# Two blocks of each feed-forward network as one seven-product step over both token tiles

## The chip, the core and the metric

The program runs on one core of one Trainium2 chip. The metric is the device time of one execution in microseconds (us). TensorE (PE) multiplies matrices, VectorE (DVE) and ScalarE (ACT) do elementwise work, GpSimd (POOL) has a handful of small operations, and SyncE (SP) issues transfers. Each engine runs its own instructions in their written order; an instruction that depends on another engine waits for a semaphore, and whatever stands behind it on that engine waits too.

## The reference

256 tokens of width 1024 pass through two layers. Each layer is a feed-forward network (FFN), a mixer (state-space branch and chunked attention) and a second FFN, all of it float32:

```python
def swiglu(h, w_gate, w_up, w_down):
    return (jax.nn.silu(h @ w_gate) * (h @ w_up)) @ w_down
...
    for l in range(DEPTH):
        g = norm_gains[l]
        f1 = swiglu(rmsnorm(x, g[0]), ffn_w_gate[l, 0], ffn_w_up[l, 0], ffn_w_down[l, 0])
        x = x + 0.5 * rmsnorm(f1, g[1])
        m = hybrid_mixer(rmsnorm(x, g[2]), w_in[l], ...)
        x = x + rmsnorm(m, g[3])
        f2 = swiglu(rmsnorm(x, g[4]), ffn_w_gate[l, 1], ffn_w_up[l, 1], ffn_w_down[l, 1])
        x = x + 0.5 * rmsnorm(f2, g[5])
```

The hidden width of an FFN is 2816; gate and up weights are 1024 x 2816, the down weight 2816 x 1024.

## The kernel before

**Tiles.** The tokens form two tiles, t = 0 and t = 1, of 128 rows. A float32 product is made of three fast ones: both operands are cut into a high part and a remainder (`hi` and `lo` for activations, `wh` and `wl` for weights), and `mm_two_k` (L468) issues hi x wh, hi x wl and lo x wh, each a 128x128 by 128x512 matmul into one bank of PSUM.

**Weights.** All weights lie in HBM as 368 chunks of 128 x 1024 (512 KB). `weight` (L443) brings one in: a transfer that SP issues into a `raw` buffer, then on ACT `wh` = raw rounded (L358), then on DVE `wl` = raw - wh (L365). There are 4 `raw` buffers and 8 each of `wh` and `wl`. Every chunk is used by both tiles, tile 1 up to three chunks behind tile 0 (`LAG`), with 6 matmuls for each tile.

**An FFN** (`ffn`, L581, called once for each tile) cuts the hidden width into six blocks, `N_BLK`, five of 512 and one of 256. For a block of 512 it takes 4 chunks of gate weights and 4 of up weights (each chunk holds 256 of the 1024 input rows), applies silu and the product (L586, L594), transposes the result into `hi` and `lo` (`t_split`), and multiplies the block before it by 4 chunks of the down weights into two banks that collect over the FFN (`gemm_wide`). A block thus has 12 chunks, 144 matmuls of 512 columns and 8 transposes. At an FFN's two ends `boundary` (L554) makes the norms and the next input, one tile after the other.

**The order** is set before anything runs. `Graph.schedule` (L197) gives every operation a due time that follows from the matmuls' places (`take`, L460) less a margin for each stream of work (`MARGIN`), lays all engines out in time with costs written into the program, buffer counts (`SLOTS`) included, and the program is emitted in the order of the start times. The chip then only keeps the order within each engine. `prep` (L622) makes constants for the state-space branch; its stream may run far ahead of its use.

Of the kernel before, what the change touches and what calls it, by code (L numbers as in the profile page):

```python
# [12 lines left out]
F32 = mybir.dt.float32  # L13
# [16 lines left out]
N_BLK = (512, 512, 512, 512, 512, 256)  # L30
FFN_CHUNKS = 66
# [4 lines left out]
SLOTS = {"blk": 28, "ps": 8, "wh": 8, "wl": 8, "raw": 4, "gain": 2,  # L36
# [4 lines left out]
MARGIN = {"conv": 7.558, "conv0": 3.423, "task": 7.748, "att0": 37.576, "s50": 37.749, "att1": 28.585, "s51": 29.753, "prep": 111.598}  # L41
# [10 lines left out]
DMA_RATE = 350e3  # L52

# [8 lines left out]
class View:  # L62
# [50 lines left out]
    def ap(self):  # L113
        t = self.buf.tile
        for s in self.steps:
            t = s(t)
        return t

# [10 lines left out]
class Graph:  # L129
# [62 lines left out]
    def latency(self, a, b):  # L192
        if a.eng == "dma":
            return DMA_LAT if b.eng != "dma" else 0.0
        return LAT.get((a.eng, b.eng), HOP)

    def schedule(self):  # L197
# [23 lines left out]
        while left:  # L221
# [90 lines left out]
class Kern:  # L312
    def __init__(self, g, x, g0, gains, wall, sp, bias, out):
# [4 lines left out]
        self.chunk = [0, 0]  # L318
        self.last_raw = None
# [46 lines left out]

    def copy(self, out, a):
# [24 lines left out]
    def mm(self, out, lhsT, rhs, start, stop):  # L392
# [3 lines left out]
        elif m == 32:  # L396
            cost = 0.05
        else:
            cost = max(0.2, n / 592)
        return self.g.op("pe", cost, [out], [lhsT, rhs], lambda: self.nc.tensor.matmul(  # L400
            out.ap(), lhsT=lhsT.ap(), rhs=rhs.ap(), start=start, stop=stop))
# [40 lines left out]

    def weight(self, i):  # L443
        if i not in self.ws:
# [3 lines left out]
            raw = g.buf("raw", [P, 1024])  # L448
            wh, wl = g.buf("wh", [P, 1024], F32R), g.buf("wl", [P, 1024], F32R)
            parts = [slice(0, 512), slice(512, 1024)] if i < 2 else [slice(0, 1024)]  # L450
            for s in parts:
                self.last_raw = self.dma(raw[:, s], self.w_d[i][:, s], after=[self.last_raw] if self.last_raw else [])
            for s in parts:
                self.act(wh[:, s], raw[:, s], AF.Copy)
                self.tt(wl[:, s], raw[:, s], wh[:, s].bitcast(F32), ALU.subtract)
            self.ws[i] = (wh, wl)
# [3 lines left out]
    def take(self, t):  # L460
# [4 lines left out]
        self.mode("main", "main", (i + t * min(LAG, 1 + i // 2)) * 2 * TAU + t * TAU)  # L465
        return w

    def mm_two_k(self, bank, xs, w, first, last):  # L468
        wh, wl = w
        for i, (xh, _) in enumerate(xs):  # L470
            s = slice(i * 512, (i + 1) * 512)
            self.mm(bank, xh, wh[:, s], first and i == 0, False)
            self.mm(bank, xh, wl[:, s], False, False)
        for i, (_, xl) in enumerate(xs):
            self.mm(bank, xl, wh[:, i * 512:(i + 1) * 512], False, last and i == len(xs) - 1)

    def gemm(self, t, xs):
# [6 lines left out]
        return bank  # L484

# [29 lines left out]
    def to_lhs(self, halves):  # L515
# [7 lines left out]
        return [p for h in range(2) for p in zip(self.cols(nh[h]), self.cols(nl[h]))]  # L523
# [6 lines left out]
    def first_norm(self, t):  # L530
# [9 lines left out]
        return [p for h in range(2) for p in zip(self.cols(nh[h]), self.cols(nl[h]))], None  # L540
# [40 lines left out]
    def ffn(self, t, l, f, normed):  # L581
        ipost = 1 if f == 0 else 5
        nxt = (l, 2) if f == 0 else (l + 1, 0)
        xs, rs = normed
        acc = (self.ps(), self.ps())
        pend, first = None, True  # L586
        for b, wd in enumerate(N_BLK):
            sil, h = self.blk(), self.blk()
            gb = self.gemm(t, xs)
            if rs is None:  # L590
                rs = self.row_scale(t, [self.g.ops[self.mark[(t, 2)]]])
            self.act(sil[:, :wd], gb[:, :wd], AF.Silu, scale=rs)
            up = self.gemm(t, xs) if wd == 512 else gb[:, wd:]
            self.stt(h[:, :wd], up, rs, sil[:, :wd], ALU.mult, ALU.mult)  # L594
# [549 lines left out]
```

## Time and profile before

| | |
|---|---|
| time, median of 3 runs | 1153.77 us (1153.56 to 1154.09) |
| profiled execution, first to last instruction | 1151.6 us |
| the same executions' time beyond the span | 1153.77 - 1151.6 = 2.2 us |
| PE busy | 1140.8 us, 99% |
| DVE busy | 788.6 us, 68% |
| ACT busy | 606.3 us, 53% |
| POOL busy | 19.8 us, 2% |
| transfers' share of the 16 DMA engines | 53.7% |

Busy is the time in which an engine had an instruction under way; matmuls are pipelined, so one lasts longer (0.4 us) than the distance to the next (some 0.23 us), and the distance is what counts.

### The profile page before, as it was taken

To read this page: it belongs to the slowest core of one execution; us is meant where nothing else is said; L and a number is where in the kernel's file an instruction comes from. 1 tells how busy PE (TensorE), PEld (TensorE's weight loads), DVE (VectorE), ACT (ScalarE), POOL (GpSimd) and SP (SyncE) were. 2 spreads that over 40 slices of the span, in tenths; PEclk is the share of its full clock that TensorE was granted. 3 is DMA by queue.
4 is the path that set the end of the run, shared out by engine and by line. 5 is a ranking of instruction groups with operands and counts; after the bars stand their busy time and mean duration, and the time that the engine had idled before them with its cause. 6 is when DMAs were issued, how large, how long until landed. Compare 5 with 4: busy or idle time off the path is not lost.

```text
span 1151.6 us, 15538 instructions
## 1 busy us (share of the span) xinstructions
PE 1140.8 (99%) x5872; PEld 914.0 (79%) x5872; DVE 788.6 (68%) x1190; ACT 606.3 (53%) x894; POOL 19.8 (2%) x53
## 2 busy tenths in 40 slices
PE   8999999999999999999999999999999999999997
PEld 7887888877788888888888878887777888888886
DVE  6995557896958854655799734578779678544553
ACT  6565445648555554444555643455685446444442
POOL 1000000000000000000000000000000000000000
PEclk9999999999999999999999999999999999999999
DMA  8754565553255665555565546654534565555551
GB/s 291 252 195 159 183 219 166 181 164 130 86 189 178 207 200 184 186 182 184 187 220 193 184 150 200 204 177 147 166 110 145 184 198 163 192 192 181 190 165 37
DMA packets 60267, 205.02 MB, mean 178 GB/s; under 512 B 7072, under 2 KB 7840, under 8 KB 60192
## 3 DMA queue, kind: packets, MB, share of 16 engines
q1 hardware_dynamic: 60192, 204.03, 53.7%
q8 instruction: 46, 0.75, 0.3%
q14 instruction: 29, 0.24, 0.1%
HBM read 202.96 MB, written 1.05 MB: 177 GB/s over the span
## 4 chain that ended last, share of the span: by engine, by line
PE 94%; ACT 4%; issue 1%; DMA 0%; SPq 0%; DVE 0%; POOLq 0%; POOL 0%; DVEq 0%
PE ps L400 89%; PE ps L414 4%; ACT utz L358 2%; PE ps L406 1%; ACT blk L358 1%; ACT wh L358 1%; DMA x<-in_x_dram 0%; SPq L341 0%; DVE x L380 0%; POOLq L1139 0%; POOL s L376 0%; DVEq L1139 0%; DVE s L388 0%; POOLq L376 0%
## 5 line engine op out<-in xcount | busy, mean ns | idle before, releaser
L400 PE MATMUL ps<-wh,blk 128*128 128x512 f32 x2944 | 916.4, 400 | 0.0
L400 PEld LDWEIGHTS ps<-wh,blk 128*128 128x128 f32 x2944 | 548.0, 188 | 122.6 <-issue 0.3
L365 DVE TENSOR_TENSOR wl<-raw,wh 128x1024 fp32r<-128x1024 f32 (+1 forms) x370 | 448.7, 1217 | 281.9 <-ACT wh L358 280.6
L358 ACT ACTIVATE wh<-raw 128x1024 fp32r<-128x1024 f32 (+1 forms) x370 | 389.7, 1055 | 374.5 <-PE ps L400 334.1
L400 PE MATMUL ps<-wl,blk 128*128 128x512 f32 x1472 | 551.7, 399 | 0.0
L400 PEld LDWEIGHTS ps<-wl,blk 128*128 128x128 f32 x1472 | 274.8, 188 | 61.1 <-issue 0.3
L358 ACT ACTIVATE blk<-ps 128x512 fp32r<-128x512 f32 (+3 forms) x136 | 78.1, 583 | 121.5 <-PE ps L414 103.3
L365 DVE TENSOR_TENSOR blk<-ps,blk 128x512 fp32r<-128x512 f32 (+2 forms) x104 | 69.0, 666 | 36.1 <-ACT blk L358 34.9
L414 PE MATMUL ps<-ident,blk 128*128 128x128 f32 x432 | 76.8, 273 | 0.2
L414 PEld LDWEIGHTS ps<-ident,blk 128*128 128x128 f32 x432 | 57.0, 140 | 20.1 <-ACT blk L358 1.0
L358 ACT ACTIVATE blk<-ps,s 128x512 f32<-128x512 f32 (+1 forms) x80 | 52.5, 658 | 27.6 <-PE ps L400 25.6
L380 DVE SCALAR_TENSOR_TENSOR blk<-ps,s,blk 128x512 f32<-128x512 f32 (+1 forms) x48 | 33.8, 703 | 15.3 <-PE ps L400 11.5
L376 POOL TENSOR_TENSOR s<-s,mhalf 128x1 f32<-128x1 f32 x24 | 13.8, 574 | 804.0 <-DVE s L388 799.1
L358 ACT ACTIVATE blk<-blk,s 128x128 f32<-128x128 f32 (+1 forms) x64 | 25.8, 444 | 0.0
L400 PEld LDWEIGHTS ps<-utz,bt 128*128 128x128 f32 x128 | 18.1, 191 | 4.0 <-ACT utz L358 2.8
L365 DVE TENSOR_TENSOR blk<-blk,blk 128x512 f32<-128x512 f32 (+3 forms) x38 | 21.1, 577 | 0.1
L358 ACT ACTIVATE utz<-blk 32x128 f32<-32x128 f32 x64 | 20.1, 314 | 1.0
L358 ACT ACTIVATE blk<-blk 64x128 f32<-64x128 f32 (+2 forms) x44 | 17.1, 393 | 6.5 <-DVE blk L380 6.0
L365 DVE TENSOR_TENSOR blk<-blk,e 128x512 f32<-128x512 f32 x32 | 20.3, 677 | 0.0
L400 PE MATMUL ps<-utz,bt 128*128 128x128 f32 x128 | 19.2, 278 | 1.0 <-ACT utz L358 0.8
L365 DVE TENSOR_TENSOR blk<-ps,e 128x512 f32<-128x512 f32 x32 | 19.9, 677 | 0.0
L856 DVE TENSOR_TENSOR_SCAN blk<-mt,blk 128x512 f32<-128x512 f32 x16 | 18.6, 1203 | 0.0
(106 smaller groups left out, 349.2 us busy)
## 6 DMA issues: line engine op xcount, KB each, us to landing
raw<-in_wall_dram SPq DMA_DIRECT2D x366, 512.0 KB, 3.5
gain<-in_gains_dram SPq DMA_DIRECT2D x22, 256.0 KB, 4.6
blk<-in_bias_dram SPq DMA_DIRECT2D x8, 256.0 KB, 5.0
raw<-in_wall_dram SPq DMA_DIRECT2D x4, 256.0 KB, 3.5
blk<-in_sp_dram SPq DMA_DIRECT2D x4, 256.0 KB, 4.0
x<-in_x_dram SPq DMA_DIRECT2D x3, 256.0 KB, 5.5
out_dram<-x SPq DMA_DIRECT2D x2, 256.0 KB, 2.0
out_dram<-x SPq DMA_DIRECT2D x2, 192.0 KB, 2.1
```

The costliest lines, as they stand in the source:

```text
L358: self.nc.scalar.activation(out=out.ap(), in_=in_.ap(), func=func, **k)
L365: lambda: self.nc.vector.tensor_tensor(out=out.ap(), in0=a.ap(), in1=b.ap(), op=op))
L376: lambda: self.nc.gpsimd.tensor_tensor(out=out.ap(), in0=a.ap(), in1=b.ap(), op=ALU.pow))
L380: return self.g.op("dve", cost, [out], [a, s, b], lambda: self.nc.vector.scalar_tensor_tensor(out=out.ap(), in0=a.ap(), scalar=ap(s), in1= ...
L400: return self.g.op("pe", cost, [out], [lhsT, rhs], lambda: self.nc.tensor.matmul(out.ap(), lhsT=lhsT.ap(), rhs=rhs.ap(), start=start, stop ...
L406: self.nc.tensor.matmul(out.ap(), lhsT=lhsT.ap(), rhs=rhs.ap(), start=start, stop=stop)
L414: lambda o=o, s=s: self.nc.tensor.transpose(o.ap(), s.ap(), self.ident.ap()))
L856: self.g.op("dve", 0.6, [o], [mt, z], lambda o=o, z=z: self.nc.vector.tensor_tensor_scan(out=o.ap(), data0=mt.ap(), data1=z.ap(), initial= ...
```

## The change

Blocks 1 and 3 of each of the four FFNs, eight blocks in all, are now computed for both tiles at once. Take the two tiles as the rows of a 2 x 2 block matrix A whose columns are the two halves of the 1024 inputs, and gate and up weights as the columns of a 2 x 2 block matrix B with the same halves as rows. The four blocks of A B (gate and up of both tiles) need 8 block products in the usual way. `seven` computes them from 7 products of sums of the blocks (Winograd's form of Strassen's scheme). A product is 12 matmuls, so a block has 84 + 48 = 132 matmuls of 512 columns in place of 96 + 48 = 144; its 8 transposes stay.

The sums of A are made once for each FFN on DVE and ACT (`sums`). The sums of B are made in the `raw` buffers: ACT multiplies four chunks by -1 in place (`minus`), and eight transfers with an adding destination, issued by POOL from SBUF to SBUF (`add_to`, 512 KB each), add chunks to chunks. Seven pairs of `wh` and `wl` are then made from the 8 loaded gate and up chunks, where there were four: 14 conversions in place of 8. The products' sums (`u2`, `u4`, `h`) are five more DVE operations on 128x512, and one ACT copy (`k1`) takes a product out of a bank that goes on collecting. `raw` has 9 buffers, `wh` and `wl` 7. Two padded buffers that were kept all along (`uTz`) are now made and cleared by POOL for each use. `prep` has a margin of 40.

```diff
+SEVEN = (((1, 3), (1, 3)), ((1, 3), (1, 3)))
-SLOTS = {"blk": 28, "ps": 8, "wh": 8, "wl": 8, "raw": 4, "gain": 2,
+SLOTS = {"blk": 28, "ps": 8, "wh": 7, "wl": 7, "raw": 9, "gain": 2,
-MARGIN = {"conv": 7.558, "conv0": 3.423, "task": 7.748, "att0": 37.576, "s50": 37.749, "att1": 28.585, "s51": 29.753, "prep": 111.598}
+MARGIN = {"conv": 7.558, "conv0": 3.423, "task": 7.748, "att0": 37.576, "s50": 37.749, "att1": 28.585, "sums": 8.0, "s51": 29.753, "prep": 40.0}
+ADD_LAT = 4.6
...
+    def add_to(self, out, in_):
+        return self.g.op("pool", 0.9, [out], [out, in_],
+                         lambda: self.nc.gpsimd.dma_start(out=out.ap(), in_=in_.ap(), accum_op=ALU.add), func="dma")
...
+    def sums(self, xs):
+        self.mode("sums", "bulk")
+        a = []
+        for t in range(2):
+            for hi, lo in xs[t].full:
+                r = self.blk()
+                self.tt(r, hi.bitcast(F32), lo.bitcast(F32), ALU.add)
+                a.append(r)
+        a11, a12, a21, a22 = a
+        self.tt(a22, a21, a22, ALU.add)
+        self.tt(a21, a11, a21, ALU.subtract)
+        self.tt(a11, a22, a11, ALU.subtract)
+        self.tt(a12, a12, a11, ALU.subtract)
+        out = []
+        for r, k in ((a22, -1.0), (a11, 1.0), (a21, 1.0), (a12, 1.0)):
+            hi, lo = self.blk(F32R), self.blk(F32R)
+            self.act(hi, r, AF.Copy, scale=k)
+            self.stt(lo, r, k, hi.bitcast(F32), ALU.mult, ALU.subtract)
+            out.append((hi, lo))
...
+    def seven(self, b, xs, rs, s, acc, pend, first):
...
+        def minus(raws):
+            for r in raws:
+                self.act(r, r, AF.Copy, scale=-1.0)
+
+        def add(to, raws):
+            for o, r in zip(to, raws):
+                self.add_to(o, r)
+
+        b11 = [self.load(i), self.load(i + 1)]
+        w1 = conv(b11)
+        self.weight(i + 2)
+        b21 = [self.load(i + 3), self.load(i + 4)]
+        w2 = conv(b21)
+        minus(b21)
+        b12 = [self.load(i + 5), self.load(i + 6)]
+        minus(b12)
+        add(b11, b12)
+        w5 = conv(b11)
+        b22 = [self.load(i + 7), self.load(i + 8)]
+        add(b12, b22)
+        add(b11, b22)
+        w6 = conv(b11)
+        self.weight(i + 9)
+        w7 = conv(b12)
+        w3 = conv(b22)
+        self.weight(i + 10)
+        add(b21, b11)
+        w4 = conv(b21)
+        self.weight(i + 11)
...
+        prod(0, p1, a11, w1, True)
+        k1 = self.blk()
+        self.act(k1, p1, AF.Copy)
+        down(2, 0)
+        prod(4, p1, a12, w2, False)
...
+        prod(6, p5, s1, w5, True)
+        prod(8, p6, s2, w6, True)
+        u2, u4 = self.blk(), self.blk()
+        self.tt(u2, p6, k1, ALU.add)
+        self.tt(u4, p5, u2, ALU.add)
+        down(10, 1)
...
+        prod(12, p7, s3, w7, True)
+        self.tt(u4, p7, u4, ALU.add)
+        prod(14, p5, s4, w3, False)
...
+        down(16, 2)
+        prod(18, p7, a22, w4, False)
...
+        down(20, 3)
+        return [self.t_split(h[t], 4) for t in range(2)]
...
+            if b in SEVEN[l][f]:
+                if s is None:
+                    s = self.sums(xs)
+                pend = self.seven(b, xs, rs, s, acc, pend, first)
...
-        self.uTz = [self.own(f"utz{i}", [P, 2, 2, 2, 64]) for i in range(2)]
+        uz = [self.blk() for _ in range(2)]
+        for z in uz:
+            self.memset("pool", z, 0.0)
```

Three pieces show how instructions stand, in block 1 of the second FFN. First POOL. In the program before, the four inverse roots of the boundaries around that block follow each other with nothing between (the four `s1` rows; the two before them clear the scan's start):

```order
L346 MEMSET st0_369_141 128x16
L346 MEMSET st1_370_143 128x16
L376 TENSOR_TENSOR s1_667_3634<-s1_666_3627,mhalf_2_74 128x1
L376 TENSOR_TENSOR s1_781_3740<-s1_780_3732,mhalf_2_74 128x1
L376 TENSOR_TENSOR s1_677_3786<-s1_676_3781,mhalf_2_74 128x1
L376 TENSOR_TENSOR s1_791_3859<-s1_790_3856,mhalf_2_74 128x1
```

Now the eight adding transfers of block 1 stand behind the last of them. raw_892 and raw_893 are the two chunks of b11, 907 and 908 those of b12, 913 and 914 of b22, 901 and 902 of b21:

```order
L391 TENSOR_TENSOR s1_835_3943<-s1_834_3936,mhalf_2_74 128x1
L380 DMA raw_892_3675<-raw_907_3793 128x1024
L380 DMA raw_893_3702<-raw_908_3814 128x1024
L380 DMA raw_907_3793<-raw_913_3854 128x1024
L380 DMA raw_908_3814<-raw_914_3941 128x1024
L380 DMA raw_892_3675<-raw_913_3854 128x1024
L380 DMA raw_893_3702<-raw_914_3941 128x1024
L380 DMA raw_901_3758<-raw_892_3675 128x1024
L380 DMA raw_902_3779<-raw_893_3702 128x1024
```

POOL has eight transfers in each of the eight blocks where it had none, and the fifth and sixth, which complete the sums for the product `w6`, come after four others.

Second PE, at block 1's second tile. Before, tile 1's gate product goes over the same weights that tile 0 used (wh_842, wh_845), between down products (ps_792 and ps_793 collect them):

```order
L400 MATMUL ps_1070_4034<-wh_842_3881,blk_782_3766 128x512
L400 MATMUL ps_1070_4034<-wl_843_3889,blk_782_3766 128x512
L400 MATMUL ps_1070_4034<-wh_842_3881,blk_782_3766 128x512
L400 MATMUL ps_1070_4034<-wl_843_3889,blk_782_3766 128x512
L400 MATMUL ps_1070_4034<-wh_842_3881,blk_784_3775 128x512 x2
L400 MATMUL ps_792_4043<-wh_857_3960,blk_823_3982 128x512
L400 MATMUL ps_793_4049<-wh_857_3960,blk_823_3982 128x512
```

Now the product on `w5` (the second chunk's pair is wh_911, wl_912) is followed at once by the first matmul on `w6` (wh_915), whose low part wl_916 comes seven matmuls later:

```order
L416 MATMUL ps_944_4120<-wh_911_4046,blk_882_3990 128x512
L416 MATMUL ps_944_4120<-wl_912_4062,blk_882_3990 128x512
L416 MATMUL ps_944_4120<-wh_911_4046,blk_883_4017 128x512 x2
L416 MATMUL ps_945_4149<-wh_915_4135,blk_884_4091 128x512
L416 MATMUL ps_836_4060<-wh_920_4058,blk_869_3998 128x512
L416 MATMUL ps_837_4064<-wh_920_4058,blk_869_3998 128x512
L416 MATMUL ps_836_4060<-wl_921_4087,blk_869_3998 128x512
L416 MATMUL ps_837_4064<-wl_921_4087,blk_869_3998 128x512
L416 MATMUL ps_836_4060<-wh_920_4058,blk_870_4010 128x512
L416 MATMUL ps_837_4064<-wh_920_4058,blk_870_4010 128x512
L416 MATMUL ps_948_4167<-wh_922_4101,blk_886_4032 128x512
L416 MATMUL ps_945_4149<-wl_916_4151,blk_884_4091 128x512
```

Behind the first `w6` matmul stand the six of a down chunk (wh_920) and one of `w7` (wh_922), and then the `w6` product goes on.

Third ACT in the same block. Before, conversions of freshly loaded chunks follow one another, each from a buffer of its own:

```order
L358 ACTIVATE wh_872_4047<-raw_871_3978 128x1024
L358 ACTIVATE blk_1065_4061<-ps_1064_4051 128x512
L358 ACTIVATE wh_875_4075<-raw_874_4006 128x1024
L358 ACTIVATE wh_878_4093<-raw_877_4021 128x1024
L358 ACTIVATE wh_881_4111<-raw_880_4045 128x1024
```

Now the two conversions for `w5` (from raw_892 and raw_893 after the first add) stand ahead of the copy `k1` out of the bank ps_940:

```order
L369 ACTIVATE wh_909_4036<-raw_892_3675 128x1024
L369 ACTIVATE wh_911_4046<-raw_893_3702 128x1024
L369 ACTIVATE blk_941_4054<-ps_940_3975 128x512
L369 ACTIVATE wh_920_4058<-raw_919_4004 128x1024
L369 ACTIVATE raw_901_3758<-raw_901_3758 128x1024
L369 ACTIVATE wh_926_4078<-raw_913_3854 128x1024
```

PE's next matmul into ps_940, the start of the product on `w2`, follows that copy.

## Rows read from the trace of the kernel before

**Rows 1.** The page's part 1: span; busy us of each engine.
```profile
span 1151.6 us, 15538 instructions
PE 1140.8 (99%) x5872; PEld 914.0 (79%) x5872; DVE 788.6 (68%) x1190; ACT 606.3 (53%) x894; POOL 19.8 (2%) x53
```

**Rows 2.** The page's part 4: the chain that ended last, shares by engine.
```profile
PE 94%; ACT 4%; issue 1%; DMA 0%; SPq 0%; DVE 0%; POOLq 0%; POOL 0%; DVEq 0%
```

**Rows 3.** Waits of the whole run: who waited for whom, us, times, longest.
```profile
ACT wh L358 <- PE ps L400: 334.1, 237, 3.0
DVE wl L365 <- ACT wh L358: 280.6, 257, 3.2
...
ACT wh L358 <- DMA raw<-in_wall_dram: 17.5, 19, 1.8
```

**Rows 4.** The chain in time, second FFN: start us, us, what.
```profile
454.25 9.02 PE ps L400 x39
...
464.18 23.74 PE ps L400 x102
...
488.58 9.09 PE ps L400 x39
...
498.57 23.70 PE ps L400 x102
...
522.94 9.03 PE ps L400 x39
```

**Rows 5.** Windows of two blocks: busy us of each engine, clock, DMA share, GB/s.
```profile
464.18:498.57 34.39, 34.39 (x153) 27.76 (x153) 21.98 (x53) 16.09 (x17) 0.00 (x0) 1.00 0.55 184
498.57:532.87 34.30, 34.30 (x153) 27.75 (x153) 17.46 (x17) 15.07 (x16) 0.00 (x0) 1.00 0.54 182
```

**Rows 6.** Groups by line and shape: busy us, mean ns, then idle before.
```profile
L365 DVE TENSOR_TENSOR wl<-raw,wh 128x1024 fp32r<-128x1024 f32 x366 | 446.0, 1223 | 278.9 <-ACT wh L358 277.7 <-issue 0.3
L358 ACT ACTIVATE wh<-raw 128x1024 fp32r<-128x1024 f32 x366 | 387.2, 1059 | 371.6 <-PE ps L400 334.1 <-issue 15.8 <-DMA raw<-in_wall_dram 14.6
...
L358 ACT ACTIVATE blk<-ps 128x512 f32<-128x512 f32 x28 | 15.8, 594 | 13.4 <-PE ps L414 9.8 <-PE ps L400 3.6
```

**Rows 7.** Timeline of DVE at a boundary: start us, us, what.
```profile
382.06 2.35 DVE L365 TENSOR_TENSOR wl<-raw,wh 128x1024 fp32r<-128x1024 f32 x2
384.33 0.68 DVE L365 TENSOR_TENSOR blk<-ps,blk 128x512 fp32r<-128x512 f32 x1
384.93 0.74 DVE L380 SCALAR_TENSOR_TENSOR blk<-blk,s,blk 128x512 f32<-128x512 f32 x1
385.59 1.22 DVE L365 TENSOR_TENSOR wl<-raw,wh 128x1024 fp32r<-128x1024 f32 x1
```

**Rows 8.** Windows around the second FFN's start, columns as in rows 5.
```profile
380.00:390.00 10.00, 10.00 (x49) 8.18 (x48) 9.63 (x15) 5.49 (x8) 0.55 (x1) 1.00 0.59 197
390.00:400.00 10.00, 10.00 (x49) 8.16 (x48) 9.65 (x15) 7.49 (x13) 1.10 (x2) 1.00 0.48 155
```

**Rows 9.** Queues and issues, whole run: share of 16 engines; KB, us to landing.
```profile
q1 hardware_dynamic: 60192, 204.03, 53.7%
...
raw<-in_wall_dram SPq DMA_DIRECT2D x366, 512.0 KB, 3.5
...
raw<-in_wall_dram SPq DMA_DIRECT2D x4, 256.0 KB, 3.5
...
out_dram<-x SPq DMA_DIRECT2D x2, 256.0 KB, 2.0
```

**Rows 10.** The same view from 10 to 60 us, the first FFN.
```profile
q1 hardware_dynamic: 4265, 13.68, 78.7%
...
raw<-in_wall_dram SPq DMA_DIRECT2D x22, 512.0 KB, 4.7
```

**Rows 11.** Windows of the first FFN, columns as in rows 5.
```profile
20.00:30.00 10.00, 10.00 (x45) 8.10 (x44) 7.54 (x17) 6.68 (x10) 0.55 (x1) 1.00 0.97 330
30.00:40.00 10.00, 10.00 (x45) 8.12 (x44) 9.61 (x32) 6.38 (x7) 0.00 (x0) 1.00 0.87 293
```

**Rows 12.** POOL's line L376: duration ns min/median/max, first and last start.
```profile
L376 POOL TENSOR_TENSOR s<-s,mhalf x24: 549/550/1108, 16.1 to 1146.4; 128x1 f32<-128x1 f32 x24
```

More of the change, by code (lines that the diff above doesn't have):

```diff
@@ L441, in cols, with load, halves @@
         return [t[:, i * P:(i + 1) * P] for i in range(n)]
+    def load(self, i, parts=(slice(0, 1024),)):
+        raw = self.g.buf("raw", [P, 1024])
+        for s in parts:
+            self.last_raw = self.dma(raw[:, s], self.w_d[i][:, s], after=[self.last_raw] if self.last_raw else [])
+        return raw
+    def halves(self, raw, parts=(slice(0, 1024),)):
+        wh, wl = self.g.buf("wh", [P, 1024], F32R), self.g.buf("wl", [P, 1024], F32R)
+        for s in parts:
+            self.act(wh[:, s], raw[:, s], AF.Copy)
+            self.tt(wl[:, s], raw[:, s], wh[:, s].bitcast(F32), ALU.subtract)
+        return wh, wl
     def weight(self, i):
@@ L447, in weight @@
             self.mode("conv" if i >= 6 else "conv0", "main")
[L448 to L456, printed above, removed]
+            parts = (slice(0, 512), slice(512, 1024)) if i < 2 else (slice(0, 1024),)
+            self.ws[i] = self.halves(self.load(i, parts), parts)
             g.stream, g.rank, g.due = keep
@@ L522, in to_lhs @@
         self.split(*trios)
-        return [p for h in range(2) for p in zip(self.cols(nh[h]), self.cols(nl[h]))]
+        return Lhs(nh, nl, [p for h in range(2) for p in zip(self.cols(nh[h]), self.cols(nl[h]))])
     def row_scale(self, t, after=()):
@@ L539, in first_norm @@
                 self.stt(lo, b, gk, hi.bitcast(F32), ALU.mult, ALU.subtract)
-        return [p for h in range(2) for p in zip(self.cols(nh[h]), self.cols(nl[h]))], None
+        return Lhs(nh, nl, [p for h in range(2) for p in zip(self.cols(nh[h]), self.cols(nl[h]))]), None
     def pre_gain(self, t, l, i):
@@ L599, in ffn @@
                     self.gain(*nxt)
-            if b == len(N_BLK) - 1:
-                pre = self.pre_gain(t, *nxt)
-            if pend is not None:
-                self.gemm_wide(t, acc, pend, first, False)
-                first = False
-            pend = res
-        self.gemm_wide(t, acc, pend, False, True)
-        return self.boundary(t, l, ipost, acc, 1.0 / 16, 4.0 * EPS, *nxt, pre)
+        out = []
+        for t in range(2):
+            self.gemm_wide(t, acc[t], pend[t], False, True)
+            out.append(self.boundary(t, l, ipost, acc[t], 1.0 / 16, 4.0 * EPS, *nxt, pre[t]))
+        return out
     def persistent(self):
```

130 lines of the change are left out of this document (100 added, 30 removed).

## The prediction

> **What bounds the kernel now.** I read the page's busy times first, then the chain that ended last, then the waits, and only then the stage that the change touches. PE is busy for 1140.8 of 1151.6 us [rows 1] and carries 94% of the chain that ended last [rows 2]; the granted clock is 1.00 in every window shown. The waits say that weights are ready early: ACT's conversions stand still for 334.1 us until PE gives a buffer back, and for only 17.5 us until a load lands [rows 3]. So the supply runs ahead as far as the buffers let it, and time is the number of matmuls times their distance. In the second FFN two whole blocks take 34.39 and 34.30 us [rows 5], and the chain's stretches put one 512-column matmul at 23.74 / 102 = 0.2327 and 23.70 / 102 = 0.2324 us [rows 4]. I use 0.2325; 144 of them are 33.5 us, and the remaining 0.9 us of a block are its 8 transposes, 0.11 us each.
>
> **The change part by part.**
>
> *Matmuls.* Each of the eight blocks loses 12, so 96 x 0.2325 = 22.3 us leave PE, which has no other work waiting. Against the profiled execution that is 1151.6 - 22.3 = 1129.3 us; with the 2.2 us by which the median stands above the span, 1131.5 us if everything added is hidden.
>
> *Conversions and sums.* A block gets 6 more ACT conversions and 4 sign changes of the same shape at 1.06 us [rows 6], and the copy `k1` at 0.59 us: 11.2 us on ACT, which had 15.1 in a block (second window of rows 5, free of `prep`). That makes 26.3 of the new block's 34.3 - 2.8 = 31.5 us. DVE's conversions last 1.22 us but start 1.13 apart, since two end after 2.35 us, and 128x512 operations start 0.60 to 0.66 us apart [rows 7]. Six conversions and five sums are 6.8 + 3.0 = 9.8 us beside the old 17.5: 27.3 of 31.5 us. Both fit, and the ordinary blocks beside them have room, so I cost them at nothing; without that cover the block would be theirs, and nothing of its 2.8 us would be left. The tightest place is an FFN's opening, where the boundary, `sums` (12 DVE operations) and block 1 meet. DVE is already at 9.63 and 9.65 of 10 us there [rows 8]. From the end of tile 1's mixer output to the low part of the last down chunk of block 1, the new order holds 22 conversions and 29 smaller operations on DVE, 24.9 + 18.5 = 43.4 us, beside 194 matmuls and 20 transposes on PE, 47.3 us. That is 92%; cost nothing, with the full durations (1.22, 0.68, 0.74) as the bound, 47.7 us or 0.4 us late.
>
> *The adding transfers.* No row shows a transfer that adds, or one that POOL issues. 53.7% of 1151.6 us moved 204.03 MB [rows 9], so a 512 KB load occupies all 16 engines for 1.59 us; it lands after 3.5 us, so 1.9 us are fixed. Call the occupation of one add a. An add delivers as many bytes as a load, which makes 1.6 us the low end. It also reads its destination: double, 3.2 us, if reads set the pace, and 4.8 us if each of the three streams costs like a load. The nearest row that starts in SBUF is the store, 256 KB landing after 2.0 us where a load of that size takes 3.5 [rows 9], so the SBUF side is the cheap one; I take a = 2.4 us and keep 1.6 and 4.8 for the range. Issue is priced at POOL's smallest instruction, 0.55 us [rows 12]. The Trainium skill ("DMA: Bandwidth & Descriptors", Anatomy of one DMA) gives about 2.0 us plus bytes / 436e3 for a plain transfer from GpSimd; no run here shows one, and as an estimate from that page 512 KB would occupy 1.2 us and the sum would be 1131.5.
>
> Who waits: on PE the low part of `w6`'s second chunk comes 20.5 us after the first matmul on `w1` in block 1 of the later FFNs (85 matmuls and 8 transposes in the second), 18.4 us in every block 3, counted in the new order. Ahead of it lie six adds, because the sums of b12 and b22 stand before the `w6` pair on POOL. The first add waits for the low part of `w1`'s first chunk, which PE wants 0.5 us in; from there 0.55 + 6a + 1.9 for the adds, 1.06 on ACT and 1.13 on DVE make 5.1 + 6a. The lateness in a block 1 is thus 6a - 15.4, plus up to 3.2 us if two loads of 1.6 us are served in between; half of that gives 6a - 13.8. At a = 2.4 the two ends are 0 and 2.2 us, and I take 1.1. In a block 3, DVE converts `w1`'s chunks ahead of two down chunks that PE wants earlier, so the first add can start some 6 us before PE reaches `w1`: 6a - 19.8, with half of three loads 6a - 17.4, nothing at a = 2.4. Other DMA traffic is the same 12 loads for each block. In the first FFN the engines are at 0.97 and 0.87 between 20 and 40 us [rows 11] and loads land after 4.7 instead of 3.5 us [rows 10]; one load and two adds in a row would each be 1.2 us later, some 3 us in all, with 0 and 6 as bounds. The Trainium skill (same page, Issuing engines are not separate DMA queues) says that transfers from every engine share the 16 engines and interleave, so it speaks for the loads' part. This trace has one data queue only and cannot show it; without sharing the time would be 1134.5.
>
> *Other edits.* The eight clearings on POOL and the later `prep` have margins of tens of microseconds and are costed at nothing. One `wh`/`wl` pair less shortens the lead by one chunk of the eight; ACT waits for PE, not for loads [rows 3], so nothing, with one chunk's late conversion (2.2 us) as the bound. An add that waits holds only later adds on POOL, since the inverse roots stand before and after the eight. ACT is more exposed: the `w5` conversions, which wait for the first two adds, stand ahead of `k1`, and PE wants `k1` 10.0 us in. The second add is ready at 3.0 + 2a, its conversion and the copy at 4.6 + 2a: 9.4 us at a = 2.4, in time.
>
> Sum: 1151.6 - 22.3 + 4 x 1.1 + 3.0 = 1136.7 us, plus 2.2: **1139 us**.
>
> **The rivals.**
>
> *Everything hidden.* An add costs like a load (a = 1.6) and even with the loads between, 6a - 12.2 is below zero: 1131.5 us. For it: the waits for loads are 17.5 us in the whole run. Against: nothing shows an add reading two streams at the price of one.
>
> *The adds become the bound, slower than before.* At the eight places PE waits for `w6`. The price is 4 x (6a - 13.8), from a = 2.9 on also 4 x (6a - 17.4), plus 3. It eats the 22.3 us at a = 3.0; at 3.2, reads at a load's price, the waits are 4 x (5.4 + 1.8) + 3 = 31.8 and the time 1163; at 4.8 they are 4 x (15.0 + 11.4) + 3 = 109 and the time 1240. For it: a transfer that reads its destination has two streams in, and during the 20 us of a block's adds the engines also hold loads. Against: the share is 0.54 in an ordinary block [rows 5], so sums over a pair of blocks fit.
>
> *The waits just return the gain.* a between 2.9 and 3.1: 1151 to 1156 us.
>
> *DVE sets the openings.* If the boundary's own waits, which leave DVE at 9.65 of 10 us at best, do not shrink, the 8% of slack are used up and block 1 starts late by some 3 us in three FFNs: 9 us on top of the forecast, 1148 us.
>
> **How the numbers follow.** Forecast 0.37, everything hidden 0.20, DVE at the openings 0.06: faster 0.63. The even case 0.09. The adds as the bound 0.28. About 0.2%, 2.3 us, is what a measurement of this kernel can tell from no change. The range starts at 1130, the full gain and 1.5 us of waits at the start that a new order may shift, and goes to 1168, a = 3.3 by the formula (4 x (6.0 + 2.4) + 3 = 36.6); a dearer add is left outside with about 0.16, and 0.03 below.
>
> **What would show it right or wrong.** 4320 matmuls of 512 columns at 0.2325 us, and blocks of 31.5 us where PE does not stand still. The landing time of the adds gives a directly (1.9 + a beyond the issue). PE's idle time should sit in front of `w6` in blocks 1, released by DVE or ACT behind an adding transfer, about 1 us each, and near nothing in blocks 3. Waits of 3 us or more there, or in front of `w2` (the copy `k1`), mean the dear add; waits for DVE without a late add mean the last rival. The prediction is wrong if an add holds the engines for 3 us or more, or if loads behind the nine `raw` buffers come late after a block.

## The result: slower by 1.25%, and the profile after

The changed kernel takes 1167.9 us (1166.6 to 1170.7), the kernel before 1153.9 in the same session: a ratio of 1.0125, 95% interval 1.0111 to 1.0140. I had forecast 1139.

The page's part 1 of the changed kernel (busy us of each engine) and its part 4 (the chain that ended last, by engine, then by line) answer to [rows 1, 2]:

```profile
span 1165.3 us, 15915 instructions
PE 1131.4 (97%) x5776; PEld 897.6 (77%) x5776; DVE 892.3 (77%) x1326; ACT 696.1 (60%) x1006; POOL 86.9 (7%) x123
...
PE 65%; DMA 13%; ACT 8%; DVE 8%; issue 5%; POOL 0%; SPq 0%; POOLq 0%; DVEq 0%; ACTq 0%
PE ps L416 61%; DMA raw<-raw 8%; ACT blk L369 4%; DMA raw<-in_wall_dram 4%; DVE wl L376 4%; ACT wh L369 3%; PE ps L430 3%; DVE blk L376 3%; PE ps L422 1%; DVE blk L1015 1%; POOL raw L380 0%; SPq L352 0%; DVE blk L395 0%; ACT L369 0%; DVE st L376 0%
```

PE's busy time fell by only 9.4 us (without the transfers, below, it is 1121.3, so 19.5 less than before) and its idle time rose from 10.8 to 33.9. On the chain PE went from 94% to 65%; the adding transfers (`raw<-raw`) alone now hold 8% of it, and loads 4%, where DMA had none. The queues and issues (share of 16 engines; KB, median us from issue to landing), as in [rows 9]:

```profile
q1 hardware_dynamic: 60192, 204.03, 50.6%
q0 software_dynamic: 9216, 33.56, 15.7%
...
raw<-in_wall_dram SPq DMA_DIRECT2D x366, 512.0 KB, 4.6
raw<-raw POOLq DMA_DIRECT2D x64, 512.0 KB, 7.5
```

An add occupies the engines for 0.157 x 1165.3 / 64 = 2.86 us; I had taken 2.4. It lands 7.5 us after its issue, where I had 2.4 + 1.9 = 4.3, and a load now takes 4.6 in place of 3.5 us (in the run without the adding transfers, below, it takes 4.4, so most of that rise is not theirs). Windows of the second FFN (busy us of each engine, clock, DMA share, GB/s), around its block 1 and then its block 3:

```profile
420.00:430.00 10.00, 10.00 (x47) 8.00 (x46) 9.25 (x12) 8.94 (x12) 2.61 (x3) 1.00 1.06 231
430.00:440.00 10.00, 8.82 (x37) 6.65 (x36) 7.58 (x9) 5.60 (x7) 1.72 (x2) 1.00 1.04 274
440.00:450.00 10.00, 9.24 (x39) 6.88 (x38) 8.30 (x10) 5.90 (x7) 0.00 (x0) 1.00 0.90 325
450.00:460.00 10.00, 10.00 (x45) 8.11 (x44) 8.30 (x9) 5.62 (x6) 0.00 (x0) 1.00 1.02 409
...
500.00:510.00 10.00, 8.71 (x37) 6.40 (x35) 9.32 (x13) 8.53 (x11) 0.00 (x0) 1.00 1.00 313
510.00:520.00 10.00, 9.19 (x33) 7.39 (x34) 8.82 (x13) 4.38 (x5) 0.00 (x0) 0.83 1.01 408
```

The engines are full while the adds run, but move only 231 to 274 GB/s; with loads alone to catch up, full engines move 409. PE stands still at both places, behind block 3 as well as block 1, and in block 1 neither DVE nor ACT is full while it does. The chain there (start us, us, what) shows that the two places wait for different things. Block 1 first, then block 3:

```profile
413.56 7.54 DMA raw<-raw
421.11 0.28 issue
421.39 0.82 POOL raw L380
422.21 11.29 DMA raw<-raw x2
...
434.04 8.10 DMA raw<-raw
442.14 0.02 issue
```
```profile
489.48 8.48 DMA raw<-in_wall_dram
497.96 0.02 issue
...
500.39 5.39 DMA raw<-in_wall_dram
505.78 0.02 issue
```

In block 1 the chain runs through the sums in a row, 27 us of landings; in block 3 it runs through plain loads, one 8.5 us old when it lands. The other FFNs show the same: in block 1 landings of sums (9.5, 7.8 and 11.4 us in the first FFN), in block 3 a load of 7.3, 9.2 and 7.9 us. PE's waits in the two places (start us, us, what; in brackets the idle time ahead of it and what ended it):

```profile
434.72 0.49 PE L416 MATMUL ps<-wh,blk 128*128 128x512 f32 x1 [0.41 <-ACT wh L369]
435.98 0.50 PE L416 MATMUL ps<-wl,blk 128*128 128x512 f32 x1 [0.76 <-DVE wl L376]
444.28 1.45 PE L416 MATMUL ps<-wh,blk 128*128 128x512 f32 x5 [0.15 <-ACT wh L369]
446.33 0.73 PE L416 MATMUL ps<-wl,blk 128*128 128x512 f32 x2 [0.60 <-DVE wl L376]
...
510.81 0.47 PE L416 MATMUL ps<-wh,blk 128*128 128x512 f32 x1 [1.95 <-DVE pt_ep L395]
```

By the order of the matmuls the first two rows are the second chunk of `w6`, the place that I had named. The next two stand behind the conversion that the landing of the last add (434.04 to 442.14) released, a place that I had not. In the last row pt_ep is a small operation of `prep`, the end of a row of DVE work behind the two loads.

For the experiments I use stage lengths, from POOL's inverse root (L391) for token tile 1 at one boundary to the next, the first from the start of the span:

```
us                          FFN 1  mixer 1  FFN 2  FFN 3  mixer 2  FFN 4
before                      208.4   182.9   190.6  195.5   182.7   186.3
changed                     215.7   186.0   192.1  196.2   186.0   184.0
side edits alone            208.7   184.6   190.5  195.5   184.5   186.5
no transfers                203.5   186.1   184.9  189.3   185.9   179.6
plain copies                207.0   186.0   184.8  189.2   186.0   179.4
copies and extra transfers  215.1   186.0   190.9  193.0   186.0   181.7
sums held by clearings      204.2   186.0   192.1  195.4   186.0   184.0
```

### The profile page after: what moved, and what is told of

The parts are those of the page before. It is cut to its first block, busy times and chain, and to the rows that moved or that the text cites. A ratio compares the mean times of both kernels' runs of the same rounds, so it can differ in the third digit from the quotient of the medians.

```text
span 1165.3 us, 15915 instructions
## 1 busy us (share of the span) xinstructions
PE 1131.4 (97%) x5776; PEld 897.6 (77%) x5776; DVE 892.3 (77%) x1326; ACT 696.1 (60%) x1006; POOL 86.9 (7%) x123
## 3 DMA queue, kind: packets, MB, share of 16 engines
q0 software_dynamic: 9216, 33.56, 15.7%
## 4 chain that ended last, share of the span: by engine, by line
PE 65%; DMA 13%; ACT 8%; DVE 8%; issue 5%; POOL 0%; SPq 0%; POOLq 0%; DVEq 0%; ACTq 0%
PE ps L416 61%; DMA raw<-raw 8%; ACT blk L369 4%; DMA raw<-in_wall_dram 4%; DVE wl L376 4%; ACT wh L369 3%; PE ps L430 3%; DVE blk L376 3%; PE ps L422 1%; DVE blk L1015 1%; POOL raw L380 0%; SPq L352 0%; DVE blk L395 0%; ACT L369 0%; DVE st L376 0%
## 5 line engine op out<-in xcount | busy, mean ns | idle before, releaser
L416 PE MATMUL ps<-wh,blk 128*128 128x512 f32 x2880 | 894.7, 401 | 16.8 <-DVE blk L376 7.5
L376 DVE TENSOR_TENSOR wl<-raw,wh 128x1024 fp32r<-128x1024 f32 (+1 forms) x418 | 500.2, 1217 | 214.6 <-ACT wh L369 212.0
L369 ACT ACTIVATE wh<-raw 128x1024 fp32r<-128x1024 f32 (+1 forms) x418 | 432.7, 1053 | 320.2 <-PE ps L416 234.2
L376 DVE TENSOR_TENSOR blk<-ps,blk 128x512 fp32r<-128x512 f32 (+2 forms) x144 | 96.1, 671 | 23.3 <-ACT blk L369 22.0
L380 POOL DMA_DIRECT2D raw<-raw x64 | 55.8, 917 | 304.8 <-ACT raw L369 172.5
L391 POOL TENSOR_TENSOR s<-s,mhalf 128x1 f32<-128x1 f32 x24 | 22.1, 919 | 549.7 <-DVE s L403 549.7
L369 ACT ACTIVATE blk<-blk 32x128 f32<-32x128 f32 (+3 forms) x132 | 52.2, 396 | 2.5 <-DVE blk L395 0.9
L376 DVE TENSOR_TENSOR blk<-blk,blk 128x512 f32<-128x512 f32 (+3 forms) x70 | 42.5, 626 | 0.2
L369 ACT ACTIVATE blk<-blk,s 128x128 f32<-128x128 f32 (+2 forms) x72 | 31.7, 472 | 8.8 <-DVE blk L376 7.7
L369 ACT ACTIVATE raw<-raw 128x1024 f32<-128x1024 f32 x32 | 33.3, 1051 | 0.2
L395 DVE SCALAR_TENSOR_TENSOR blk<-blk,s,blk 128x512 f32<-128x512 f32 x36 | 26.6, 747 | 2.8 <-ACT blk L369 2.7
L395 DVE SCALAR_TENSOR_TENSOR blk<-blk,blk 128x512 fp32r<-128x512 f32 (+2 forms) x38 | 21.6, 575 | 0.5 <-ACT blk L369 0.4
L376 DVE TENSOR_TENSOR blk<-blk,e 128x512 f32<-128x512 f32 x32 | 20.3, 679 | 0.0
```

The source lines that it names most:

```text
L369: self.nc.scalar.activation(out=out.ap(), in_=in_.ap(), func=func, **k)
L376: lambda: self.nc.vector.tensor_tensor(out=out.ap(), in0=a.ap(), in1=b.ap(), op=op))
L380: lambda: self.nc.gpsimd.dma_start(out=out.ap(), in_=in_.ap(), accum_op=ALU.add), func="dma")
L391: lambda: self.nc.gpsimd.tensor_tensor(out=out.ap(), in0=a.ap(), in1=b.ap(), op=ALU.pow))
L395: return self.g.op("dve", cost, [out], [a, s, b], lambda: self.nc.vector.scalar_tensor_tensor(out=out.ap(), in0=a.ap(), scalar=ap(s), in1= ...
```

## The experiments

**What costs: the transfers, the added work on ACT and DVE, or the side edits?** Theory T says the adding transfers, rival C the conversions and sums, rival S the side edits. The side edits alone:

```diff
-SEVEN = (((1, 3), (1, 3)), ((1, 3), (1, 3)))
+SEVEN = (((), ()), ((), ()))
```


> No block is computed from quadrants (all 528 weight tiles go the old way, 8 products); kept are the other edits of the change: 7 buffers each for the upper and lower weight halves in place of 8, 9 raw buffers in place of 4, the cleared block buffers in the mixers, the later preparation, both token tiles walked in one function. Theory T (the 64 accumulating transfers are what costs: each holds the 16 engines 2.86 us and lands 7.5 us after its issue, so sums and loads come late): the FFNs run as before, and only the 6.4 us that the two mixers lost remain, if they come from these edits: 1153.9 + 6.4 = about 1160; 1154 if the mixers' loss is an aftermath of the transfers instead. Rival S (these side edits cost most of the loss, in the FFNs too: 36 us against the 1131 with everything hidden): 1175 to 1190, slower than the changed kernel.

Measured 1157.3 us, 1.0030 of before (1.0019 to 1.0041). The table has these 3.5 us in the two mixers; the FFNs are as before. Rival S falls as the main cause.

The transfers alone left out:

```diff
         def add(to, raws):
-            for o, r in zip(to, raws):
-                self.add_to(o, r)
+            pass
```


> The changed kernel without its 64 accumulating transfers: the sums of the weights are not formed, and the products use the loaded quadrants in their place; every conversion, sum of the tokens, sign change and matmul stays. Theory T: the 29 to 30 us that the four FFNs lost come back: 1167.9 - 30 = about 1138, with the DMA share in the new blocks back near 0.8. Rival C (the added conversions and sums on ScalarE and VectorE are late): the stalls stay, 1160 to 1168. Rival S (side edits): 1160 to 1168 as well, but then the kernel with the side edits alone is slow too.

Measured 1136.4 us, 0.9850 of before (0.9833 to 0.9866): 31.5 us come back, 30.6 of them in the FFNs. All conversions, token sums and matmuls are still there, so rival C falls.

**The adding, or the moving of bytes?** The same transfers without the adding:

```diff
-                         lambda: self.nc.gpsimd.dma_start(out=out.ap(), in_=in_.ap(), accum_op=ALU.add), func="dma")
+                         lambda: self.nc.gpsimd.dma_start(out=out.ap(), in_=in_.ap()), func="dma")
```


> The changed kernel with its 64 transfers from buffer to buffer as plain copies of the same 512 KB (no adding, so the weights' sums are wrong in value; all else the same). If what costs is moving the bytes through the shared engines and the fixed way of a transfer, copies cost as the adding ones: occupation 2.6 to 2.9 us, landing about 7 us, time 1165 to 1168. If it is the adding that is slow, occupation falls towards what a load of the same 512 KB takes by the share of the hardware queue (0.506 x 1165.3 x 16 engines for 204.03 MB: 1.5 us of all 16), landing to about 4.6 us, and the time to 1140 to 1150.

Measured 1140.4 us, 0.9881 (0.9866 to 0.9895). Queue and issue of the copies:

```profile
q0 software_dynamic: 9216, 33.56, 7.5%
...
raw<-raw POOLq DMA_DIRECT2D x64, 512.0 KB, 3.5
```

Same packets, same bytes, half the share: 0.075 x 1139.1 / 64 = 1.33 us, and 3.5 us to the landing. The adding doubles both, 2.86 and 7.5, and is worth 27.5 of the 31.5 us; of the 4.0 us that the copies cost, 3.5 lie in the first FFN.

**Engine time, or waiting for the sums?** First, as much engine time, on transfers nobody waits for. To the kernel with copies:

```diff
-                self.add_to(o, r)
+                q = self.add_to(o, r)
+                n = self.n_extra
+                self.n_extra += 1
+                self.g.op("dma", 0.0, [], [], lambda n=n: self.nc.sync.dma_start(out=self.scratch[n], in_=self.w_d[n]),
+                          after=[q])
```


> The kernel with plain copies in place of the adding transfers (1140.4 us; a copy holds the engines 1.33 us and lands in 3.5), plus one more transfer of 512 KB per copy, from memory to memory on the hardware queue, that nothing waits for. The engines are then held about as long per sum as by the adding (2.7 to 3.0 us in place of 2.86), but no sum is waited for longer by itself. If it is the engines' time that made the changed kernel late (loads and sums crowded out): 1160 to 1170. If it is the four landings in a row, 7.5 us each, that the last sum waits for: 1140 to 1147. The values are as wrong as with the copies.

Measured 1159.3 us (1155.3 to 1161.1), 1.0045 (1.0029 to 1.0062), just below what engine time was to give:

```profile
q1 hardware_dynamic: 62240, 237.59, 59.3%
q0 software_dynamic: 9216, 33.56, 7.3%
...
raw<-raw POOLq DMA_DIRECT2D x64, 512.0 KB, 6.9
```

A copy holds the engines for 1.32 us, an extra transfer for (0.593 x 1159.3 - 0.515 x 1139.1) / 64 = 1.58 (51.5% was that queue's share with the copies alone), together 2.90 us per sum. But beside the extra transfers the copies' own landing rose from 3.5 to 6.9 us, so this run did not keep the two apart. The opposite run has no transfer at all: two sums hold POOL for eight clearings of 0.96 us, 7.7 us, about as long as a landing.

```diff
-                         lambda: self.nc.gpsimd.dma_start(out=out.ap(), in_=in_.ap(), accum_op=ALU.add), func="dma")
+        def fn():
+            for _ in range(4):
+                self.nc.gpsimd.memset(out.ap(), 0.0)
+        return self.g.op("pool", 0.9, [out], [out, in_], fn, func="dma")
```


> The changed kernel with each adding transfer replaced by four clearings of the same 128x1024 buffer on GpSimd, one after the other (the sum is lost, its buffer and all who wait for it stay): no transfer, but a sum comes some 4 us after its issue, its half behind it some 8, so the four sums in a row last about as long as the four landings of 7.5 us. If waiting for the sums is what made the changed kernel late, 1155 to 1168 as it. If it was the engines' time that the loads lacked, 1136 to 1143, as without the transfers (1136.4) or with the copies (1140.4).

Measured 1154.1 us, 1.0002 (0.9993 to 1.0012), between the two expectations. By stages, FFNs 2 to 4 take 192.1, 195.4, 184.0 us, as the changed kernel (192.1, 196.2, 184.0), and the first takes 204.2, as without transfers (203.5). But that the lengths agree is chance, as the places show. The next table has by how much PE falls behind the kernel without transfers, from the starts of the same matmul, counted in PE's order, in both traces: from an FFN's start to the end of its block 1, and from there to the FFN's end, where block 3 lies.

```
us                          FFN 1        FFN 2        FFN 3        FFN 4
                            to 1  then   to 1  then   to 1  then   to 1  then
changed                     10.7   1.5    3.1   4.1    4.0   2.7    3.6   0.8
copies and extra transfers   7.7   4.1    1.4   4.5    1.8   1.8    2.3  -0.1
sums held by clearings       0.1   0.0    4.7   2.5    6.1  -0.2    4.6  -0.1
```

In block 1 of FFNs 2 to 4, sums that come late are enough, with no transfer: the clearings cost 15.4 us there (part of the 6.1 in the third is a stretch at a lower clock, 0.98 over that stage), the changed kernel loses 10.7. Behind block 1 it is different: the changed kernel loses 7.6 us there, the copies with extra transfers 6.2, and the clearings 2.5, in the second FFN alone, where the chain of that run goes through small operations of `prep` on DVE. So most of block 3's loss needs the transfers' time on the engines, as its chain through loads says. In the first FFN the clearings cost nothing either: its loss needs the transfers too, though its chain runs through the sums, which land there after 9.5, 7.8 and 11.4 us, later than the clearings held them. Windows of the first FFN of the changed kernel, of the copies with extra transfers, and of this run:

```profile
40.00:70.00 30.00, 22.83 (x90) 17.04 (x91) 21.32 (x25) 18.37 (x21) 5.26 (x6) 0.97 1.04 281
```
```profile
40.00:70.00 30.00, 25.76 (x100) 19.58 (x101) 22.22 (x33) 18.18 (x21) 2.68 (x5) 0.94 0.95 374
```
```profile
40.00:70.00 30.00, 30.00 (x131) 24.27 (x130) 28.16 (x43) 20.48 (x24) 15.58 (x17) 1.00 0.85 290
```

At a share of 1.04 PE is busy for 22.8 of 30 us, at 0.85 for all of it.

**Which block pays?** One new block in each FFN:

```diff
-SEVEN = (((1, 3), (1, 3)), ((1, 3), (1, 3)))
+SEVEN = (((3,), (3,)), ((3,), (3,)))
```


> Block 3 alone of each FFN from quadrants: 48 matmuls and 32 adding transfers fewer than before and in the changed kernel. If every new block pays the same, half of the 31.5 us that leaving the transfers out gave back remain: 1136.4 + 11.2 (48 matmuls at 0.2325 more than both blocks) + 15.7 = 1163. If a new block pays because another stands one block ahead of it (loads not caught up), a single one with old blocks on both sides pays little: 1147.6 + 0 to 4 = 1148 to 1152. If only block 1 had paid, as my forecast had it, also 1148.

> Block 1 alone of each FFN from quadrants, with 32 adding transfers. Block 3 alone cost 7 us over what it would without transfers (1154.6 against 1136.4 + 11.2 = 1147.6), both together 31.5. If the blocks pay each for itself, block 1 pays the other 24.5: 1147.6 + 24.5 = 1172. If the price of both comes from the two following each other (the engines have one old block to catch up), block 1 alone pays about 7 as block 3 does, and 3 more in the first FFN: 1154 to 1158. My forecast's own formula for block 1, 6a - 13.8 with a = 2.86, gives 3.4 x 4 + 3 = 17: 1164.

> Block 2 alone of each FFN from quadrants, 32 adding transfers, all else as in the kernels with block 3 alone (1154.6) or block 1 alone (1168.9). If block 1 pays more because the FFN's opening stands just ahead of it (the token sums of 1024 columns and the boundary's work fill VectorE, and in the first FFN the loads still run behind): block 2 has a whole old block between and pays as block 3, 1152 to 1157. If it pays by the place in the plan in some other way, block 2 lies between: 1158 to 1168.

With (1,) and (2,) in the same place the others. Measured: block 3 alone 1154.6 us (1.0012, 1.0001 to 1.0022), block 1 alone 1168.9 (1.0132, 1.0117 to 1.0148), block 2 alone 1152.6 (0.9994, 0.9985 to 1.0003). With one block and no transfers it would be 1136.4 + 48 x 0.2325 = 1147.6 us, so block 3 pays 7.0, block 1 21.3 and block 2 5.0 us; 7.0 + 21.3 is close to the 31.5 of both, so in the main each pays for itself; the table above has 21.4 us up to the end of block 1 and 9.1 behind it. That block 2 pays little speaks for the FFN's opening as the reason at block 1, though it doesn't show which part of it. Above all it is the first FFN: of the 16.3 us between block 1 alone and block 2 alone, 10.1 lie there (217.0 against 206.9 by its stage).

**Can another order of the same work help?** The planner is told that an add holds the loads' engine:

```diff
             free[e] = o.end
+            if o.func == "dma":
+                free["dma"] = max(free["dma"], o.end) + ADD_OCC
+                o.lat = free["dma"] + ADD_LAT - ADD_OCC - o.end
```


> The changed kernel, with the planner told that an adding transfer holds the loads' engine for 2.9 us (it knew of no occupation, 4.6 us to the landing); buffers and work are unchanged, the order of loads, sums and conversions is laid out anew. If a wrong order was the fault, most of the 31.5 us comes back: 1140 to 1150. If the engines cannot carry 12 loads of 1.5 us and 8 sums of 2.86 us (41 us) in a block of 31.5 us with 9 buffers to run ahead in, an order changes little: 1160 to 1175.

Measured 1185.4 us, 1.0269 (1.0249 to 1.0289): worse, beyond the upper end. The largest waits of PE:

```profile
PE ps L420 <- DVE blk L380: 29.2, 11, 6.5
PE ps L420 <- DVE wl L380: 6.4, 10, 0.8
```

The adds cost as much (15.7%, 7.6 us). A better model gave a worse order; why PE then waits for DVE's small operations I did not settle, and a still better order is not ruled out.

**The sums on another engine.** On GpSimd, as elementwise adds:

```diff
-        return self.g.op("pool", 0.9, [out], [out, in_],
-                         lambda: self.nc.gpsimd.dma_start(out=out.ap(), in_=in_.ap(), accum_op=ALU.add), func="dma")
+        return self.g.op("pool", 2.3, [out], [out, in_],
+                         lambda: self.nc.gpsimd.tensor_tensor(out=out.ap(), in0=out.ap(), in1=in_.ap(), op=ALU.add))
```


> The 64 sums as elementwise adds of 128x1024 on GpSimd in place of transfers; no row so far shows the time of one. Theory T: the DMA engines carry the loads alone (share near 0.8 in the new blocks, as before), and if one add takes under 3.5 us (the four in a row on the way to the last sum then take 14 us, less than the four landings of 7.5 us now), the stalls shrink: 1138 to 1145. If one takes 5 us or more, the chain is as long as now: 1160 or more though the engines are free. Rivals C and S: 1160 to 1168 whatever the adds take.

Measured 1225.9 us, 1.0624 (1.0608 to 1.0640). An add takes 2.98 us, under the 3.5 that I had named as good enough, and yet (groups by line and shape: busy us, mean ns):

```profile
L376 DVE TENSOR_TENSOR wl<-raw,wh 128x1024 fp32r<-128x1024 f32 (+1 forms) x418 | 576.8, 1402 | 161.7 <-ACT wh L369 158.1
...
L380 POOL TENSOR_TENSOR raw<-raw,raw 128x1024 f32<-128x1024 f32 x64 | 189.1, 2979 | 233.8 <-DVE wl L376 130.1
```

DVE's conversions went from 1.22 to 1.40 us in the mean over the run, 76.5 us more in all than with the clearings above. That this is the whole of the 89.5 us by which the kernel is later than without transfers is not shown. In the run with the clearings POOL was busier still and DVE was not slower:

```profile
L376 DVE TENSOR_TENSOR wl<-raw,wh 128x1024 fp32r<-128x1024 f32 (+1 forms) x418 | 500.3, 1218 | 196.7 <-ACT wh L369 193.0 <-DMA gain<-in_gains_dram 1.5
...
L381 POOL MEMSET raw<- 128x1024 f32 x256 | 241.4, 956 | 132.1 <-DVE wl L376 121.1
```

The Trainium skill ("SBUF — State Buffer", SBUF: two separate sides) says that an operation of VectorE with two inputs in SBUF and one of GpSimd that reads SBUF exclude each other. Both rows agree: the add reads, the clearing doesn't.

On VectorE, in block 3 alone, with 8, 8 and 7 buffers:

```diff
-SEVEN = (((1, 3), (1, 3)), ((1, 3), (1, 3)))
+SEVEN = (((3,), (3,)), ((3,), (3,)))
...
-                self.add_to(o, r)
+                if self.nadd in DVE_ADDS:
+                    self.tt(o, o, r, ALU.add)
+                else:
+                    self.add_to(o, r)
+            self.nadd += 1
```


> Block 3 alone from quadrants, its sums as adds on VectorE (32 of 128x1024, 1.22 us each by the conversions' row) and no adding transfer at all; 8 buffers each for the weight halves and 7 raw ones. Without the transfers nothing crowds the loads; what could bind instead is VectorE: 27.3 + 8 x 1.22 = 37 us in a block of 31.5. If its neighbours take up those 5.6 us: 1153.9 - 11.2 + 0 to 3 (mixers) = 1143 to 1146, faster than before. If they don't: 4 x 5.6 = 22 later, 1160 to 1166.

`DVE_ADDS` holds all four sums. Measured 1142.5 us (1141.7 to 1142.9), 0.9903 of before (0.9888 to 0.9918): faster than both kernels. Part 1 of its page, and windows of block 3 of the second FFN:

```profile
PE 1129.1 (99%) x5824; PEld 906.6 (79%) x5824; DVE 888.2 (78%) x1314; ACT 656.4 (58%) x962; POOL 23.1 (2%) x59
```
```profile
490.00:500.00 10.00, 10.00 (x45) 8.13 (x44) 9.83 (x11) 6.57 (x8) 0.00 (x0) 1.00 0.88 293
500.00:510.00 10.00, 10.00 (x45) 8.10 (x44) 9.63 (x9) 6.04 (x6) 0.00 (x0) 1.00 0.99 357
```

DVE is nearly full there and PE never waits. The floor for it, with no sums at all:

> Block 3 alone from quadrants with no sums of weights formed at all (so the products use the loaded quadrants), 8 and 8 and 7 buffers: the floor for the kernel that adds on VectorE (1142.45). If those 32 adds are hidden in VectorE's idle time, the same 1142 to 1143. If they cost something on the path, up to 1.22 x 32 = 39 less; 1153.5 - 11.2 = 1142.3 is what the matmuls alone give, so under 1140 isn't expected.

Measured 1144.3 us, 0.9919 (0.9902 to 0.9935), not below the kernel that does form its sums: the 32 adds are hidden. Both blocks in this way:

> Blocks 1 and 3 from quadrants, all 64 sums as adds on VectorE (1.22 us each), no adding transfer, 8 buffers each for the weight halves and 7 raw ones: block 3 alone in this form took 1142.45. If VectorE has room for block 1 as well: 1142.5 - 11.2 = 1131 to 1134. If VectorE is the bound there (37 us of work in a block of 31.5, and the token sums and the boundary of the FFN just ahead of block 1), block 1 gives back what block 3 gained or more: 1150 to 1170.

Measured 1163.4 us, 1.0084 (1.0069 to 1.0099). Windows of block 1 of its second FFN:

```profile
420.00:430.00 10.00, 7.80 (x33) 5.71 (x31) 10.00 (x14) 3.53 (x5) 0.00 (x0) 1.00 0.16 55
430.00:440.00 10.00, 6.82 (x17) 5.04 (x18) 10.00 (x9) 7.80 (x8) 0.00 (x0) 0.66 0.76 247
```

DVE is full, PE stands still and the granted clock falls to 0.66 over 10 us. So in the orders tried block 1 has room for its sums neither on the DMA engines nor on VectorE.

**What the mixers lost.** The side edits alone, with 8, 8 and 4 buffers again:

```diff
-SLOTS = {"blk": 28, "ps": 8, "wh": 7, "wl": 7, "raw": 9, "gain": 2,
+SLOTS = {"blk": 28, "ps": 8, "wh": 8, "wl": 8, "raw": 4, "gain": 2,
```


> As the kernel with the side edits alone (1157.3 us; 7 buffers each for the weight halves, 9 raw), but with 8, 8 and 4 as before the change. If the missing eighth buffers cost the 3.5 us (the mixers 1.7 each): 1153.5 to 1154.5. If it is the later preparation or the block buffers cleared in the mixers: 1157 again.

Measured 1154.7 us, 1.0008 (0.9999 to 1.0017), mixers 183.2 and 183.0: the missing eighth pair of buffers costs each mixer 1.4 to 1.5 us. It is not the number of `raw` buffers, 4 here and 9 there: with 8, 8 and 7 (sums on VectorE, block 3 alone) the mixers take 183.2 and 183.1. In the changed kernel each mixer's stage is another 1.5 us longer, but that is no loss: between the same marks PE executes 1152 and 1151 matmuls, with the side edits alone 1146. In the kernels with block 1 from quadrants five or six matmuls of the FFN behind (6 x 0.2325 = 1.4 us) stand ahead of the mark, and the FFN stages together are shorter by as much.

## Why the prediction was wrong

*Matmuls: right.* Without transfers the kernel takes 20.9 us less than with the side edits alone (1136.4 against 1157.3); I had 22.3. (By stages the FFNs are 24.0 us shorter, but 3.0 of these only moved into the mixers' stages.)

*Conversions and token sums at nothing: right,* by the same kernel, to the 1.4 us between the two figures. The rival of DVE at the openings did not come about through them; with eight more adds there it does.

*The adding transfers: the step that failed,* in size and in what waits for them. The value of a, 2.4, was taken because it was nearest to the store, a transfer that doesn't add. The copy (1.33 us) confirms that row: the side of SBUF is cheap, and the adding is what costs, which the store could not show. With 2.86 my own formula gives 4 x (6 x 2.86 - 13.8) + 3 + 1131.5 = 1148 us, still faster: a accounts for 9 of the 29 us by which I was off. In block 1 of FFNs 2 to 4 that formula has the right size, 3.4 us at 2.86 where the table has 3.1, 4.0 and 3.6. Some of that is luck. In the second FFN 1.7 us are lost in front of `w6`, as I had it, and 1.3 behind the last add, which the formula left out. For the sums up to `w6` I added six occupations and one fixed tail of 1.9 us: 0.55 + 6 x 2.4 + 1.9 = 16.9, or 19.6 at 2.86. There it was 21.2 us, from the first add's issue (412.43) to the conversions that a landing released (433.61), since the fifth and sixth adds first wait for a whole landing (7.5 us) and then land 11.3 us later.

The larger error is what the formula had no term for: in it loads delay adds, but no load comes late because of the adds. Behind block 1, where I had nothing (and the formula at 2.86 has nothing), FFNs 2 to 4 lose 7.6 us, and the chain there runs through loads; in the first FFN the adds cost 5.7 us more than formula and allowance (3.4 + 3.0) give. Late loads behind the nine `raw` buffers were the second of the signs that I had named for being wrong. SP's queue also waits for adds to free `raw` buffers; what these waits alone cost is not shown (who waited for whom: us, times, longest):

```profile
SPq L352 <- DMA raw<-in_wall_dram: 53.5, 12, 8.9
SPq L352 <- DMA raw<-raw: 52.9, 12, 12.4
```

So block 3, which I had at nothing, pays 7.0 us by itself.

*The first FFN: right place, wrong size.* I had 3 us for it beside the 1.1 of its block 1; it lost 12.1, where its engines were already at 0.97 and 0.87 [rows 11] and eight adds of 2.86 us in block 1 went on top; the clearings, which need no transfer, cost nothing there.

*Other edits at nothing: wrong* by 3.5 us, above the bound of 2.2 that I had named for the buffers, of which the eighth pair is 2.6 (1157.3 against 1154.7); the mixers pay it, and I had looked at the FFNs only.

*The rival that came true* was the adds as the bound. Its point of decision, a = 3.0, was too high by the same error: at 2.86 the kernel is slower than before. For the even case I also read my formula wrongly: a between 2.9 and 3.1 gives 1149 to 1159 us, not 1151 to 1156.

*On the pages named:* the copies give what I could not have before. The Trainium skill ("DMA: Bandwidth & Descriptors", Anatomy of one DMA) has 2.0 + 1.2 = 3.2 us for a plain transfer of 512 KB from GpSimd; the copy takes 3.5 and occupies 1.33, so the trace agrees, for copies. The Trainium skill's other rule (same page, Issuing engines are not separate DMA queues), that transfers from every engine share the 16 engines, is borne out as well: transfers on SP's queue took POOL's copies from 3.5 to 6.9 us.

## What to carry to other kernels

A transfer that adds is not a transfer with something for free: here it cost twice a copy in engine time and in landing. Price a row of dependent ones by whole landings, and ask also which loads come late behind them. Before work moves to an engine or queue that looks half idle over the whole run, look at its share in the very stretch: here 0.55 in an ordinary block became 1.0, while VectorE, with the higher share, took the sums of a later block for nothing. Where two of something are changed, try each alone: one of the two blocks was worth its saving, the other paid three times as much as its neighbour. And when an experiment gives the same time as the kernel that it is to explain, look whether it loses the time in the same places: the clearings gave the same stage lengths with the losses elsewhere.

## What the hardware showed that I had not expected

- An adding transfer of 512 KB within SBUF occupied the 16 engines for 2.86 us and landed after 7.5 us; the same copy 1.33 and 3.5. Issuing it kept POOL busy for 0.92 us in the mean, the copy for 0.54.
- An elementwise add of 128x1024 on GpSimd took 2.98 us against 1.22 on VectorE, and raised VectorE's mean for its own two-input operation from 1.22 to 1.40 us. A clearing on GpSimd (0.96 us) did not.
- The granted clock fell behind longer waits of PE: 0.83 between 510 and 520 us of the changed kernel, behind the wait of 1.95 us shown above, and 0.66 in the window above where PE stood still for 3.2 of 10 us. Full is 2.4 GHz, so part of these windows ran at 1.2. In the first case matmuls started 0.43 us apart for some 3 us, and that cost 1.6 us on top of the wait: a stall can cost more than its own length.
